# First norm's sums moved to TensorE and the last adaLN pair to VectorE in a one-core encoder layer

## The chip, the cores and the metric

The kernel runs on one core of one Trainium2 chip. The metric is device microseconds of one execution. Of the kernel before three runs were timed: 2474.91, 2477.87 and 2481.15 us, median 2477.87. One more execution was taken with the hardware profiler.

## The reference, cut to what matters

One encoder layer is applied to two requests of 256 tokens with D = 2048, laid side by side as 512 columns. The part around the change is the first adaLN-modulated RMSNorm and the product with `w_in`:

```
def rms_norm(x, g):
    y = x * rsqrt(mean(x * x, axis=-1, keepdims=True) + 1e-6)
    return y * g

def encoder_layer(x, c, w_ada, b_ada, norm1_g, w_in, ...):
    mod = silu(c) @ w_ada + b_ada                       # c: one row for each request
    sh1, sc1, gt1, sh2, sc2, gt2 = split(mod, 6)        # 2048 columns each
    hn = rms_norm(x, norm1_g) * (1 + sc1) + sh1
    h = hn @ w_in                                       # 6496 columns: RWKV-7 group, short-conv group
    ...                                                 # delta-rule scan in both directions, conv, gates
    x = x + gt1 * (concat([y_rwkv, y_conv]) @ w_out)
    hn = rms_norm(x, norm2_g) * (1 + sc2) + sh2
    ff = (silu(hn @ w_ffn_gate) * (hn @ w_ffn_up)) @ w_ffn_down
    return x + gt2 * ff                                 # and a last rms_norm
```

## The kernel before

Activations lie with features on the 128 partitions and the 512 tokens along the free axis, so x is 16 feature tiles `xt[k]` of 128x512. A product in nearly full precision is made of three matmuls of fp32r operands: each operand is split into a rounded high part and the low rest, and `products` issues high*high, high*low and low*high (a "group of three" below). The split of a 128x512 piece of weights is one ScalarE copy and one VectorE subtraction.

**The head** is the first 150 us or so. `ADA0` (line 42) lists the feature tiles of the first norm in the order in which their shift and scale columns of `w_ada` are worked out: tiles 0 and 1 alone, then six pairs, then tiles 14 and 15 alone. For each entry `ada_blocks` loads blocks of 512 KB into a ring of six buffers (g13, g14, g15, g18, g19, g20) and multiplies them by silu(c) in bank 6 (`ada_mm`); these are matmuls of plain fp32 with 32 rows of output. `ada_sum` copies the bank out with ScalarE and turns the sums into columns with small matmuls; `ada_mod` adds the biases (three small VectorE instructions into `md`) and then makes the two halves of `hn[k]`: two ScalarE activations of 128x256 with scale and bias, one ScalarE copy to the rounded part, one VectorE subtraction.

Between the entries stands `stream`, which multiplies the finished tiles with the 7 output tiles of `w_in0`: 7 groups of three matmuls for each feature tile, into 7 PSUM banks that stay open until tile 15. So the head holds 112 groups, and no bank can be read before tile 15 has been added. A raw block of `w_in0` holds 8 of these weights; there are three raw buffers and four buffers for split weights (h0 to h3).

`load_x` (line 662) loads x in eight pieces, squares each tile on ScalarE into two scratch halves of g9, and adds the squares up on VectorE into `sqa`, 15 additions one after the other. `rms` (line 564) sums `sqa` over the partitions with four matmuls against a column of ones, takes the root (one ScalarE instruction, some small VectorE instructions) and spreads the result over the partitions with four more matmuls. The result is copied to `rst`, and VectorE multiplies each of the 16 tiles by it in place.

**After the head** come eight passes over head pairs, each with a scan (`core`), with products of `w_in` as filling, then `w_out`, the second norm (`norm2`), the FFN and the last norm. Nine more groups of adaLN columns are worked out on VectorE meanwhile, 32 instructions each: `ada_rest` (line 759) loads `w_ada` in halves of 256 KB into `aw` and adds them, scaled by silu(c), into `aacc`; eight matmuls and a transposition then make columns of it (`asum`). The last of these groups is needed by `norm2`, whose tiles are made by `hn2_half` (line 1183) in one step: normed and scaled on VectorE, shifted and rounded on ScalarE, low part on VectorE.

**What sets the order.** Nothing is issued in the order of the code. All instructions are recorded as nodes with a cost and a priority (a lower number goes first); `Program.schedule` (line 239) runs a list scheduler over them and writes each engine's queue in the order of its planned starts. Each engine then works through its queue strictly in order, SyncE's queue of DMAs too. The planner holds a model of the DMA engines, one transfer after the other at 360 KB per us (line 328). Squares, the norm and the head's columns have priority 2 (`S_CORE`), splits of weights 0 (`S_SPLIT`), evacuations 1 (`S_EVAC`), VectorE's adaLN columns 8 (`S_ADA`), the groups of three 9 (`S_MAIN`).

Of the kernel before, what the change touches and what calls it, by code (L numbers as in the profile page):

```python
# [11 lines left out]
F32 = mybir.dt.float32  # L12
F32R = mybir.dt.float32r
AF = mybir.ActivationFunctionType
ALU = mybir.AluOpType
# [26 lines left out]
ADA0 = ((0, 1), (1, 1)) + tuple((k, 2) for k in range(2, 14, 2)) + ((14, 1), (15, 1))  # L42
# [154 lines left out]
class Program:  # L197
# [41 lines left out]
    def schedule(self):  # L239
# [24 lines left out]
        while done < n:  # L264
# [62 lines left out]
            if nbytes:  # L327
                dma_free = max(dma_free, end + 0.65) + nbytes / 360e3
                end = dma_free + 0.8
# [18 lines left out]
def hymba_layer_kernel(ctx: ExitStack, tc: tile.TileContext, xT, par, cst, w_ada0, w_ada1, w_in0, w_in1,  # L348
# [215 lines left out]
    def rms(sqacc, ps, psb, out, rs, prio, w0=0, w1=4):  # L564

        n = w1 - w0
        pe([mm(ps[:, w:w + 1], sqacc[:, 128 * w:128 * w + 128], ones, 1) for w in range(w0, w1)], prio)
        var, r, t = (rs[:, 4 * i + w0:4 * i + w1] for i in range(3))
        ts(var, ps[:, w0:w1], RMS_EPS, ALU.add, n, prio, fast=False)
        act(r, var, AF.Sqrt, n, prio)  # L570
        recip(r, r, n, prio)
        newton(r, var, t, n, prio)
        pe([mm(psb[:, 128 * w:128 * w + 128], r[:, w - w0:w - w0 + 1].to_broadcast([128, 128]), ident, 128)
            for w in range(w0, w1)], prio)
        if out is not None:
            acopy(out, psb, T, prio)
# [63 lines left out]

    def ada_mod(k0, nk):
        pt = bank[6]
        ada_sum(pt, g[11][:, 512 * (k0 // 2 % 2):512 * (k0 // 2 % 2) + 256 * nk], pt, 256 * nk, S_EVAC)
        m = pt[:, 0:4 * nk].rearrange("p (k a q) -> p a k q", a=2, q=2)
# [4 lines left out]
        for k in range(k0, k0 + nk):  # L649
            x, f = xt[k], g[10][:, 512 * (k % 2):512 * (k % 2) + 512]  # L650
            for q in range(2):
                s = slice(TQ * q, TQ * q + TQ)
                act(f[:, s], x[:, s], AF.Identity, TQ, S_EVAC, scale=md[:, 1, k, q:q + 1], bias=md[:, 0, k, q:q + 1])
            acopy(hn[k][:, 0:T], f, T, S_EVAC)
            tt(hn[k][:, T:], f, hn[k][:, 0:T].bitcast(F32), ALU.subtract, T, S_EVAC)
# [6 lines left out]
    def load_x():  # L662
# [3 lines left out]
        for k in range(KT):  # L666
            sumsq(xt[k], g[9][:, 512 * (k % 2):512 * (k % 2) + 512], sqa, k == 0, S_CORE)
        rms(sqa, bank[5], bank[5], rst, rs4, S_CORE)
        for k in range(KT):
            tt(xt[k], xt[k], rst, ALU.mult, T, S_CORE)  # L670
# [78 lines left out]
    for i, (k0, nk) in enumerate(ADA0):  # L749
        ada_blocks(k0, nk)  # L750
# [4 lines left out]
        ada_mod(k0, nk)  # L755
    stream(lambda i: w_in0[i], head, at=at, prio=S_HEAD)


    def ada_rest(gi, slots=None, prio=S_ADA):
# [9 lines left out]
        else:  # L769
            for kk in range(KT):  # L770
                w = wide["aw"][:, 512 * (kk % 2):512 * (kk % 2) + 512]
                dma(w, w_ada1[gi, kk // 2, :, 512 * (kk % 2):512 * (kk % 2) + 512], 1 << 18, S_ADA,
                    after=[hn[KT - 1]] if gi == 0 and kk < 2 else [])
                for q in range(2):
                    c = wide["aacc"][:, T * q:T * q + T]
                    if kk == 0:
                        ts(c, w, sil[:, kk, q:q + 1], ALU.mult, T, S_ADA)
                    else:
                        stt(c, w, sil[:, kk, q:q + 1], c, ALU.mult, ALU.add, T, S_ADA)
            a = wide["aacc"].rearrange("p (q j e i) -> p e q j i", q=2, j=4, e=4)  # L780
            pe([mm(ps[32 * e:32 * e + 32, 128 * q:128 * q + 128], unit, a[:, e, q], 128)
                for q in range(2) for e in range(4)], S_MISC)
            tr32(asum, ps[:, 0:256], 256, S_MISC)
# [809 lines left out]
```

## Time and profile before

| what | before |
|---|---|
| median of three runs | 2477.87 us |
| the profiled execution, its own time | 2481.56 us |
| its span, first to last instruction | 2479.7 us |
| TensorE busy | 2418.7 us, 98% |
| VectorE busy | 1911.8 us, 77% |
| ScalarE busy | 1112.5 us, 45% |
| share of TensorE in the chain that ended last | 86% |
| mean granted TensorE clock | 0.993 |

The span and what lies around it differ by 1.9 us. A busy TensorE is not TensorE at its peak, since the ends of matmuls are modelled; an idle stretch in brackets at the end of a timeline row names the engine and tile that ended it. In timeline rows `x8` counts records, and a plain fp32 matmul leaves two of them, so that four such matmuls read `x8` or somewhat less where a record is missing.

### The profile page before, as it was taken

The page shows a single profiled execution, that of the slowest core. Times are in us where ns is not written, and L with a number is a line of the kernel's source. Part 1 is how long each engine was busy: PE and PEld are TensorE (multiplying, and loading weights), DVE is VectorE, ACT ScalarE, POOL GpSimd, SP SyncE. Part 2 cuts the span into 40 slices and gives each one's busy share as a digit, 9 for nine tenths or more (in the row PEclk, how much of TensorE's full clock was granted, in tenths as well). Part 3 has the DMA queues.
Part 4 walks back from the last instruction along what each step waited for, and adds up shares of the span by engine and source line. Part 5 has one row for each costly group of instructions (what it writes and reads, how often), then busy time and mean ns, then how long its engine had stood idle before and what let it go on. Part 6 is the DMA issues. An engine that isn't in the chain of part 4 may idle for free.

```text
span 2479.7 us, 46341 instructions
## 1 busy us (share of the span) xinstructions
PE 2418.7 (98%) x18220; PEld 2066.7 (83%) x18220; DVE 1911.8 (77%) x3511; ACT 1112.5 (45%) x1848; POOL 12.5 (1%) x42
## 2 busy tenths in 40 slices
PE   5999999999999999989999999999999999999997
PEld 3578777777777777688999999999999988788887
DVE  4279988889889897795888888888888887734356
ACT  4465745745646643364444444444444433223232
POOL 0000000000000000000000000000000000000000
PEclk9999999999999999999999999999999999999998
DMA  9953434434434748733333333333333476533343
GB/s 344 357 163 125 146 120 135 148 130 138 152 119 141 235 133 285 273 109 103 128 112 128 120 120 120 117 122 114 126 111 128 161 230 201 197 112 127 120 139 115
DMA packets 188233, 384.66 MB, mean 155 GB/s; under 512 B 36336, under 2 KB 51056, under 8 KB 188016
## 3 DMA queue, kind: packets, MB, share of 16 engines
q1 hardware_dynamic: 188016, 381.72, 46.1%
q8 instruction: 142, 2.33, 0.4%
q14 instruction: 75, 0.61, 0.1%
HBM read 355.03 MB, written 28.18 MB: 155 GB/s over the span
## 4 chain that ended last, share of the span: by engine, by line
PE 86%; DVE 5%; DMA 5%; ACT 2%; issue 1%; SPq 0%; DVEq 0%; ACTq 0%
PE b L374 86%; DVE g L405 2%; DMA aw<-in_w_ada_dram 1%; ACT g L396 1%; DVE h L405 1%; DVE g L410 1%; DVE aacc L410 1%; DMA g<-hrvar 1%; DMA w<-in_w_out_dram 1%; PE b L385 1%; DMA g<-hrpre 1%; DMA w<-in_w_gu_dram 0%; DMA g<-hrmean 0%; ACT L396 0%; DMA hrmean<-rowm 0%
## 5 line engine op out<-in xcount | busy, mean ns | idle before, releaser
L374 PE MATMUL b<-r,h 128*128 128x512 f32 (+1 forms) x4920 | 1130.5, 375 | 4.8 <-ACT r L396 2.5
L374 PEld LDWEIGHTS b<-r,h 128*128 128x128 f32 x4920 | 856.1, 189 | 191.9 <-issue 28.8
L396 ACT ACTIVATE h<-w 128x512 fp32r<-128x512 f32 (+2 forms) x587 | 391.8, 670 | 643.2 <-PE b L374 572.9
L374 PE MATMUL b<-g,h 128*128 128x256 f32 (+1 forms) x3452 | 654.1, 332 | 0.5 <-DVE rowp L418 0.2
L405 DVE TENSOR_TENSOR h<-w,h 128x512 fp32r<-128x512 f32 (+3 forms) x595 | 432.6, 729 | 227.4 <-ACT h L396 215.1
L374 PEld LDWEIGHTS b<-g,h 128*128 128x128 f32 x3452 | 534.0, 190 | 73.8 <-issue 11.2
L374 PE MATMUL b<-g,g 128*128 128x256 f32 (+4 forms) x5372 | 427.2, 241 | 4.0 <-DVE g L405 2.9
L374 PEld LDWEIGHTS b<-g,g 128*128 128x128 f32 (+4 forms) x5372 | 354.1, 152 | 48.7 <-issue 25.6
L410 DVE SCALAR_TENSOR_TENSOR aacc<-aw,sil,aacc 128x512 f32<-128x512 f32 x390 | 276.5, 744 | 50.5 <-DMA aw<-in_w_ada_dram 49.2
L396 ACT ACTIVATE g<-g 128x1024 fp32r<-128x1024 f32 (+6 forms) x268 | 204.2, 763 | 247.0 <-DVE aacc L405 102.6
L405 DVE TENSOR_TENSOR g<-g,g 128x512 f32<-128x512 f32 (+24 forms) x681 | 253.8, 380 | 29.0 <-ACT g L396 12.8
L374 PE MATMUL b<-r,g 128*128 128x256 f32 x1412 | 269.5, 283 | 1.5 <-ACT r L396 1.3
L396 ACT ACTIVATE g<-b 32x128 f32<-32x128 f32 (+3 forms) x454 | 174.9, 390 | 167.3 <-PE b L374 141.2
L374 PEld LDWEIGHTS b<-r,g 128*128 128x128 f32 x1412 | 214.2, 191 | 1.9 <-ACT r L396 1.4
L374 PE MATMUL b<-g,r 128*128 128x256 f32 x748 | 194.7, 281 | 0.0
L374 PE MATMUL b<-r,r 128*128 128x256 f32 x700 | 189.0, 281 | 0.0
L405 DVE TENSOR_TENSOR g<-g,b 128x256 f32<-128x256 f32 (+1 forms) x300 | 146.1, 498 | 34.1 <-PE b L374 26.9
L405 DVE TENSOR_TENSOR r<-aacc,g 128x1024 fp32r<-128x1024 f32 x80 | 97.8, 1223 | 60.3 <-ACT g L396 60.3
L396 ACT ACTIVATE g<-aacc 128x1024 fp32r<-128x1024 f32 (+1 forms) x82 | 86.1, 1050 | 129.2 <-PE b L374 127.2
L405 DVE TENSOR_TENSOR r<-g,g 128x1024 fp32r<-128x1024 f32 x80 | 97.7, 1222 | 48.3 <-ACT g L396 48.3
L374 PEld LDWEIGHTS b<-g,r 128*128 128x128 f32 x748 | 134.2, 188 | 0.1
L374 PEld LDWEIGHTS b<-r,r 128*128 128x128 f32 x700 | 128.2, 188 | 0.0
(113 smaller groups left out, 1215.7 us busy)
## 6 DMA issues: line engine op xcount, KB each, us to landing
w<-in_w_gu_dram SPq DMA_DIRECT2D x240, 256.0 KB
aw<-in_w_ada_dram SPq DMA_DIRECT2D x208, 256.0 KB
w<-in_w_in_dram SPq DMA_DIRECT2D x102, 512.0 KB
w<-in_w_down_dram SPq DMA_DIRECT2D x88, 512.0 KB
g<-in_w_ada_dram SPq DMA_DIRECT2D x80, 512.0 KB
aw<-in_w_gu_dram SPq DMA_DIRECT2D x80, 256.0 KB
w<-in_w_out_dram SPq DMA_DIRECT2D x32, 512.0 KB
act<-g SPq DMA_DIRECT2D x44, 256.0 KB
```

The lines of the kernel that those rows point to most:

```text
L374: return [nc.tensor.matmul(R(out), lhsT=R(l), rhs=R(r), start=start, stop=stop) for out, l, r, n, start, stop, one in mms]
L385: return [nc.tensor.transpose(R(out), R(i), R(idn)) for out, i, idn in items]
L396: lambda: nc.scalar.activation(out=R(out), in_=R(in_), func=func, scale=R(scale), bias=R(bias)),
L405: lambda: e.tensor_tensor(out=R(out), in0=R(a), in1=R(b), op=op), [a, b], [out], prio)
L410: lambda: e.scalar_tensor_tensor(out=R(out), in0=R(a), scalar=R(s), in1=R(b), op0=op0, op1=op1),
```

## The change

- **Squares.** The squares of tiles 3, 6, 9, 11, 13 and 15 (`SQ_PE`) are no longer added on VectorE but summed over the partitions by TensorE, four matmuls against the column of ones for each tile, into the four columns of bank 5 that the sums of `sqa` go to; `rms` then adds those of `sqa` (`begun`). VectorE keeps 9 of the 15 additions. The scratch has four halves (g9 and g10) in place of two. `rms` of the first norm has priority 0 in place of 2.
- **One step.** The 16 multiplications of x by `rst` are gone. `ada_mod` makes each half tile with one VectorE instruction (x times scale times `rst`), one ScalarE activation (plus shift, rounded) and one VectorE instruction (low part), all of 128x256.
- **Tiles 14 and 15.** Their columns are worked out on VectorE by `ada_rows`, the code of `ada_rest` made common: 8 blocks of 512 KB into six buffers that the scan uses later (g12, g16, g17, g21, g22, g23), loaded at priority 8 once `hn[7]` is there, 32 instructions into `aacc`, then the eight matmuls and the transposition (`ada_columns`). The ring's matmuls for these two tiles are gone. The same bytes are loaded.
- **The list.** `ADA0` now has tiles 0 to 3 alone and then six pairs.
- **The planner** reckons with 390 KB per us in place of 360 for every DMA of the program, so that the order changes after the head too.

```diff
-ADA0 = ((0, 1), (1, 1)) + tuple((k, 2) for k in range(2, 14, 2)) + ((14, 1), (15, 1))
+ADA0 = ((0, 1), (1, 1), (2, 1), (3, 1)) + tuple((k, 2) for k in range(4, 16, 2))
+ADA0_DVE = {14: 7}
+SQ_PE = (3, 6, 9, 11, 13, 15)
...
-                dma_free = max(dma_free, end + 0.65) + nbytes / 360e3
+                dma_free = max(dma_free, end + 0.65) + nbytes / 390e3
...
-        pe([mm(ps[:, w:w + 1], sqacc[:, 128 * w:128 * w + 128], ones, 1) for w in range(w0, w1)], prio)
+        pe([mm(ps[:, w:w + 1], sqacc[:, 128 * w:128 * w + 128], ones, 1, not begun, not begun or w + 1 == w1)
+            for w in range(w0, w1)], prio)
...
+    def ada_rows(row, prio, after=(), blocks=None):
+        for kk in range(KT):
+            c = slice(512 * (kk % 2), 512 * (kk % 2) + 512)
+            if blocks is None:
+                w = wide["aw"][:, c]
+                dma(w, row(kk), 1 << 18, prio, after=after if kk < 2 else ())
+            else:
+                b = blocks[kk // 2 % len(blocks)]
+                w = b[:, c]
+                if kk % 2 == 0:
+                    dma(b, row(kk), 1 << 19, prio, after=after)
+            for q in range(2):
+                c = wide["aacc"][:, T * q:T * q + T]
+                if kk == 0:
+                    ts(c, w, sil[:, kk, q:q + 1], ALU.mult, T, prio)
+                else:
+                    stt(c, w, sil[:, kk, q:q + 1], c, ALU.mult, ALU.add, T, prio)
+    def ada_columns(ps, prio):
+        a = wide["aacc"].rearrange("p (q j e i) -> p e q j i", q=2, j=4, e=4)
+        pe([mm(ps[32 * e:32 * e + 32, 128 * q:128 * q + 128], unit, a[:, e, q], 128)
+            for q in range(2) for e in range(4)], prio)
+        tr32(asum, ps[:, 0:256], 256, prio)
     def ada_mod(k0, nk):
         pt = bank[6]
-        ada_sum(pt, g[11][:, 512 * (k0 // 2 % 2):512 * (k0 // 2 % 2) + 256 * nk], pt, 256 * nk, S_EVAC)
-        m = pt[:, 0:4 * nk].rearrange("p (k a q) -> p a k q", a=2, q=2)
+        if k0 in ADA0_DVE:
+            ada_columns(pt, S_EVAC)
+            m = asum.rearrange("p (q k a i) -> p a k q i", q=2, k=2, a=2)[:, :, :, :, 0]
+        else:
+            ada_sum(pt, g[11][:, 512 * (k0 // 2 % 2):512 * (k0 // 2 % 2) + 256 * nk], pt, 256 * nk, S_EVAC)
+            m = pt[:, 0:4 * nk].rearrange("p (k a q) -> p a k q", a=2, q=2)
...
-            x, f = xt[k], g[10][:, 512 * (k % 2):512 * (k % 2) + 512]
+            x, f = xt[k], g[9 + k // 2 % 2][:, 512 * (k % 2):512 * (k % 2) + 512]
             for q in range(2):
                 s = slice(TQ * q, TQ * q + TQ)
-                act(f[:, s], x[:, s], AF.Identity, TQ, S_EVAC, scale=md[:, 1, k, q:q + 1], bias=md[:, 0, k, q:q + 1])
-            acopy(hn[k][:, 0:T], f, T, S_EVAC)
-            tt(hn[k][:, T:], f, hn[k][:, 0:T].bitcast(F32), ALU.subtract, T, S_EVAC)
+                stt(f[:, s], x[:, s], md[:, 1, k, q:q + 1], rst[:, s], ALU.mult, ALU.mult, TQ, S_EVAC)
+                act(hn[k][:, s], f[:, s], AF.Identity, TQ, S_EVAC, bias=md[:, 0, k, q:q + 1])
+            for q in range(2):
+                s = slice(TQ * q, TQ * q + TQ)
+                stt(hn[k][:, T + TQ * q:T + TQ * q + TQ], f[:, s], md[:, 0, k, q:q + 1], hn[k][:, s].bitcast(F32),
+                    ALU.add, ALU.subtract, TQ, S_EVAC)
...
         for k in range(KT):
-            sumsq(xt[k], g[9][:, 512 * (k % 2):512 * (k % 2) + 512], sqa, k == 0, S_CORE)
-        rms(sqa, bank[5], bank[5], rst, rs4, S_CORE)
-        for k in range(KT):
-            tt(xt[k], xt[k], rst, ALU.mult, T, S_CORE)
+            t = g[9 + k // 2 % 2][:, 512 * (k % 2):512 * (k % 2) + 512]
+            if k in SQ_PE:
+                act(t, xt[k], AF.Square, T, S_CORE)
+                pe([mm(bank[5][:, w:w + 1], t[:, 128 * w:128 * w + 128], ones, 1, k == SQ_PE[0] and w == 0, False)
+                    for w in range(4)], S_CORE)
+            else:
+                sumsq(xt[k], t, sqa, k == 0, S_CORE)
+        rms(sqa, bank[5], bank[5], rst, rs4, S_SPLIT, begun=True)
...
-        ada_blocks(k0, nk)
+        if k0 not in ADA0_DVE:
+            ada_blocks(k0, nk)
...
+        for c, k in ADA0_DVE.items():
+            if k0 <= k < k0 + nk:
+                ada_rows(lambda kk: w_ada0[4 * c + kk // 2], S_ADA, [hn[k]], [g[i] for i in (12, 16, 17, 21, 22, 23)])
```

The queues that the change moves are shown at three places. In names, `g`, `h`, `b` and `r` with their first number are buffers, split weights, PSUM banks and tiles of `hn`; `x4` counts instructions.

TensorE's queue at the start, before: `g13` to `g20` are the ring's blocks times silu(c), `128x1` are the sums of the squares, `rs4` spreads the result, `r0` opens the products of tile 0.

```order
L374 MATMUL b6_293<-g13_243,sil32_205 32x256 x4
L374 MATMUL b5_298<-cs_199,g8_241 128x1 x4
L374 MATMUL b6_293<-g14_245,sil32_205 32x256 x4
L374 MATMUL b6_293<-g15_250,sil32_205 32x256 x4
L374 MATMUL b6_293<-g18_253,sil32_205 32x256 x4
L374 MATMUL b5_298<-cs_199,rs4_308 128x128 x4
L374 MATMUL b6_293<-cs_199,g11_330 32x2 x8
L374 MATMUL b6_293<-g19_256,sil32_205 32x256 x4
L374 MATMUL b6_293<-g20_260,sil32_205 32x256 x4
L374 MATMUL b6_293<-g13_243,sil32_205 32x256 x4
L374 MATMUL b0_385<-r0_374,h0_346 128x512 x3
L374 MATMUL b1_392<-r0_374,h0_346 128x512 x3
```

The same place after the change; ahead of it stand the sums of tiles 3, 6, 9, 11 and 13.

```order
L379 MATMUL b6_309<-g15_250,sil32_205 32x256 x4
L379 MATMUL b6_309<-g18_255,sil32_205 32x256 x4
L379 MATMUL b5_264<-cs_199,g10_252 128x1 x4
L379 MATMUL b5_264<-cs_199,g8_241 128x1 x4
L379 MATMUL b6_309<-cs_199,g11_333 32x2 x8
L379 MATMUL b6_309<-g19_258,sil32_205 32x256 x4
L379 MATMUL b6_309<-g20_261,sil32_205 32x256 x4
L379 MATMUL b5_264<-cs_199,rs4_348 128x128 x4
L379 MATMUL b6_309<-g13_243,sil32_205 32x256 x4
L379 MATMUL b6_309<-g14_246,sil32_205 32x256 x4
L379 MATMUL b6_309<-cs_199,g11_333 32x2 x8
L379 MATMUL b0_415<-r0_400,h0_364 128x512 x3
```

The last sums stood behind one of tile 0's four blocks and now stand behind all four; tile 0's products stood behind the third block of tile 1 and now stand behind its fourth and its sums. On VectorE the two low parts of `h0` and `h1` now stand between the small instructions of the root, where they stood behind them.

TensorE's queue from the column sums (`g11`, 32x2) of tiles 10 and 11 on, before, up to the tenth row after them; tile 10 follows after four more rows.

```order
L374 MATMUL b6_293<-cs_199,g11_330 32x2 x16
L374 MATMUL b7_456<-r8_822,h3_368 128x512 x3
L374 MATMUL b6_293<-g13_243,sil32_205 32x512 x2
L374 MATMUL b6_293<-g14_245,sil32_205 32x512 x2
L374 MATMUL b0_385<-r9_834,h3_368 128x512 x3
L374 MATMUL b1_392<-r9_834,h0_346 128x512 x3
L374 MATMUL b6_293<-g15_250,sil32_205 32x512 x2
L374 MATMUL b6_293<-g18_253,sil32_205 32x512 x2
L374 MATMUL b2_398<-r9_834,h0_346 128x512 x3
L374 MATMUL b3_409<-r9_834,h0_346 128x512 x3
L374 MATMUL b4_426<-r9_834,h0_346 128x512 x3
```

The same place after the change, to the first products of tile 10.

```order
L379 MATMUL b6_309<-g20_261,sil32_205 32x512 x2
L379 MATMUL b3_456<-r9_865,h0_364 128x512 x3
L379 MATMUL b4_471<-r9_865,h0_364 128x512 x3
L379 MATMUL b6_309<-cs_199,g11_333 32x2 x16
L379 MATMUL b5_264<-r9_865,h1_369 128x512 x3
L379 MATMUL b7_497<-r9_865,h1_369 128x512 x3
L379 MATMUL b0_415<-r10_1020,h1_369 128x512 x3
```

Two groups of three stand between the sums of tiles 10 and 11 and the first use of tile 10, where eight stood.

VectorE's queue around the last adaLN group (`aacc`, `asum`) and the second norm, before; `g21` with `r8` and bank 7 is the first tile of the second norm.

```order
L410 SCALAR_TENSOR_TENSOR aacc_1172<-aw_1150,sil_222,aacc_1172 128x512
L410 SCALAR_TENSOR_TENSOR g7_10045<-g20_260,md_342,g7_10045 128x256
L405 TENSOR_TENSOR aw_10049<-w2_270,aw_10049 128x512
L441 STREAM_TRANSPOSE asum_2193<-b5_298 128x256
L405 TENSOR_TENSOR md_342<-asum_2193,ba1_234 128x8
L405 TENSOR_TENSOR aacc_10061<-w2_270,aacc_10061 128x512
L405 TENSOR_TENSOR md_342<-md_342,pm_207 128x8
L410 SCALAR_TENSOR_TENSOR g21_1218<-r8_7855,md_342,b7_456 128x256
```

After the change; the root of the second norm's first half follows two rows further on.

```order
L415 SCALAR_TENSOR_TENSOR aacc_813<-aw_1208,sil_222,aacc_813 128x512
L410 TENSOR_TENSOR h2_373<-w1_273,h2_373 128x512
L410 TENSOR_TENSOR h3_377<-w1_273,h3_377 128x512
L410 TENSOR_TENSOR aw_9917<-w2_275,aw_9917 128x512
L415 SCALAR_TENSOR_TENSOR r15_8012<-b4_471,md_351,r15_8012 128x256
L410 TENSOR_TENSOR aacc_9933<-w2_275,aacc_9933 128x512
L410 TENSOR_TENSOR g23_790<-g23_790,g20_261 128x256
L446 STREAM_TRANSPOSE asum_1160<-b5_264 128x256
L410 TENSOR_TENSOR md_351<-asum_1160,ba1_234 128x8
L410 TENSOR_TENSOR md_351<-md_351,pm_207 128x8
```

The last column instruction and the transposition stood behind the root of the second norm's first half and behind tiles made from it; now they stand ahead of that root. On TensorE the group's eight matmuls stood right ahead of the sums of the second half; now they stand 14 rows ahead of the sums of the first half.

## Rows read from the trace of the kernel before

**Rows 1.** Busy time by stretch. Columns: the stretch in us from the span's start, its length, then busy time (and instructions) of TensorE, its weight loads, VectorE, ScalarE and GpSimd, then the granted TensorE clock as a share of full speed, the busy share of the DMA engines and GB/s.

```profile
0.00:30.00 30.00, 9.61 (x88) 5.58 (x88) 15.17 (x35) 16.97 (x29) 1.38 (x9) 1.00 0.95 364
30.00:54.00 24.00, 19.39 (x139) 9.97 (x139) 13.83 (x28) 8.12 (x16) 0.00 (x0) 0.92 0.94 335
54.00:155.00 101.00, 100.72 (x702) 60.56 (x703) 34.31 (x70) 41.83 (x74) 0.17 (x2) 0.99 0.80 290
155.00:1000.00 845.00, 832.34 (x7203) 648.65 (x7202) 736.62 (x1540) 471.25 (x933) 10.94 (x31) 1.00 0.49 155
1000.00:1100.00 100.00, 91.57 (x685) 73.25 (x684) 86.41 (x187) 47.04 (x98) 0.00 (x0) 0.95 0.62 211
```

**Rows 2.** The timeline of the first norm on all engines: start, duration, engine, line, operation, tiles, count of records, and in brackets the idle time before it and what ended it.

```profile
17.59 1.08 PE L374 MATMUL b<-g,sil 128*32 128x256 f32 x8 [17.59 <-DMA g<-in_w_ada_dram]
...
19.87 1.78 PEld L374 LDWEIGHTS b<-cs,g 128*128 128x128 f32 x8 [2.08 <-DVE g L405]
19.87 1.87 PE L374 MATMUL b<-cs,g 128*128 128x1 f32 x8 [1.20 <-DVE g L405]
...
23.02 0.16 DVE L405 TENSOR_TENSOR rs<-rs 128x4 f32<-128x4 f32 x1
...
24.39 2.06 PE L374 MATMUL b<-cs,rs 128*128 128x128 f32 x8
...
26.49 0.60 ACT L396 ACTIVATE g<-b 128x512 f32<-128x512 f32 x1 [1.58 <-PE b L374]
...
28.40 2.49 DVE L405 TENSOR_TENSOR h<-w,h 128x512 fp32r<-128x512 f32 x4
...
29.02 0.64 PE L374 MATMUL b<-g,sil 128*32 128x256 f32 x8 [0.84 <-DMA g<-in_w_ada_dram]
```

**Rows 3.** The same timeline from the first products on, with TensorE's idle stretches and VectorE's in-place scaling.

```profile
32.01 6.70 DVE L405 TENSOR_TENSOR g<-g,g 128x512 f32<-128x512 f32 x11
...
32.15 3.00 PE L374 MATMUL b<-r,h 128*128 128x512 f32 x8 [0.79 <-DVE r L405]
...
37.19 0.31 PE L374 MATMUL b<-cs,g 128*32 128x2 f32 x16
...
38.91 1.92 PE L374 MATMUL b<-g,sil 128*32 128x512 f32 x16 [0.51 <-DVE md L405]
...
50.18 0.43 PE L374 MATMUL b<-cs,g 128*32 128x2 f32 x32 [0.74 <-ACT g L396]
...
51.05 1.07 PE L374 MATMUL b<-g,sil 128*32 128x512 f32 x8 [0.43 <-DVE md L405]
...
53.36 0.69 DVE L405 TENSOR_TENSOR r<-g,r 128x512 fp32r<-128x512 f32 x1 [2.17 <-ACT r L396]
...
53.38 4.16 PE L374 MATMUL b<-r,h 128*128 128x512 f32 x9 [1.27 <-ACT r L396]
```

**Rows 4.** Granted clock of the stretch after the last of these idle times, in the columns of rows 1.

```profile
54.00:56.00 2.00, 1.90 (x5) 1.51 (x6) 0.74 (x2) 0.48 (x1) 0.00 (x0) 0.50 0.76 289
```

**Rows 5.** TensorE's timeline over a pair of tiles, over tiles 14 and 15 and at the end of the head (columns as in rows 2).

```profile
100.70 1.07 PE L374 MATMUL b<-g,sil 128*32 128x512 f32 x8
101.69 3.70 PE L374 MATMUL b<-r,h 128*128 128x512 f32 x15
...
122.82 1.07 PE L374 MATMUL b<-g,sil 128*32 128x256 f32 x16
...
125.40 0.64 PE L374 MATMUL b<-g,sil 128*32 128x256 f32 x8
...
126.86 0.64 PE L374 MATMUL b<-g,sil 128*32 128x256 f32 x8
...
128.32 0.31 PE L374 MATMUL b<-cs,g 128*32 128x2 f32 x16
...
136.58 17.97 PE L374 MATMUL b<-r,h 128*128 128x512 f32 x78
```

**Rows 6.** Prices on VectorE and TensorE that the new instructions are nearest to: the first two rows are forms of VectorE's line 410 (count, shortest, median and longest duration in ns), the last is TensorE's timeline at one group's eight column matmuls.

```profile
L410 DVE SCALAR_TENSOR_TENSOR aacc<-aw,sil,aacc x390: 647/745/754, 145.6 to 2154.9; 128x512 f32<-128x512 f32 x195
...
L410 DVE SCALAR_TENSOR_TENSOR r<-g,md,r x16: 464/476/483, 1073.9 to 1098.0; 128x256 fp32r<-128x256 f32 x16
...
  DMA aw<-in_w_ada_dram: 49.2, 53
...
255.61 0.62 PE L374 MATMUL b<-aacc,cs 128*32 128x128 f32 x16
```

**Rows 7.** TensorE's timeline at the second norm (columns as in rows 2), and under the dots the granted clock of one stretch in the columns of rows 1.

```profile
1079.56 0.43 PE L374 MATMUL b<-aacc,cs 128*32 128x128 f32 x8 [0.34 <-DVE aacc L410]
1081.93 0.43 PE L374 MATMUL b<-aacc,cs 128*32 128x128 f32 x8 [1.94 <-DVE aacc L410]
1083.67 0.61 PE L374 MATMUL b<-cs,g 128*128 128x1 f32 x4 [1.32 <-DVE asum L441]
1085.61 0.58 PE L374 MATMUL b<-r,g 128*128 128x256 f32 x1 [1.33 <-ACT r L396]
1086.38 3.99 PE L374 MATMUL b<-r,g 128*128 128x256 f32 x17 [0.19 <-DVE r L410]
...
1090.88 3.84 PE L374 MATMUL b<-r,g 128*128 128x256 f32 x30
...
1086.00:1088.00 2.00, 1.81 (x8) 1.62 (x8) 2.00 (x9) 2.00 (x7) 0.00 (x0) 0.50 0.59 223
```

More of the change, by code (lines that the diff above doesn't have):

```diff
@@ L561, in mtile, with rms @@
                  (lambda: done(ps)) if k == n - 1 else None) for k in range(n)]
-    def rms(sqacc, ps, psb, out, rs, prio, w0=0, w1=4):
+    def rms(sqacc, ps, psb, out, rs, prio, w0=0, w1=4, begun=False):
         n = w1 - w0
-        pe([mm(ps[:, w:w + 1], sqacc[:, 128 * w:128 * w + 128], ones, 1) for w in range(w0, w1)], prio)
+        pe([mm(ps[:, w:w + 1], sqacc[:, 128 * w:128 * w + 128], ones, 1, not begun, not begun or w + 1 == w1)
+            for w in range(w0, w1)], prio)
         var, r, t = (rs[:, 4 * i + w0:4 * i + w1] for i in range(3))
@@ L769, in ada_rest @@
         else:
[L770 to L783, printed above, removed]
+            ada_rows(lambda kk: w_ada1[gi, kk // 2, :, 512 * (kk % 2):512 * (kk % 2) + 512], S_ADA,
+                     [hn[KT - 1]] if gi == 0 else ())
+            ada_columns(ps, S_MISC)
         kind, k0 = 2 + gi // 4, 4 * (gi % 4)
```

## The prediction, made before the changed kernel ran

> **What bounds the kernel now.** I first read busy time by stretch [rows 1]. From 155 us on TensorE is idle for 12.7 of 845 us up to 1000 and for 8.4 of the 100 us after that. In the head it is idle for 20.4 of the first 30 us and 4.6 of the next 24, and then for 0.3 of 101. The DMA engines are 95, 94 and 80% busy in these three stretches: transfers set the first 30 us, and TensorE's own work sets the head from 54 us on. So the change can gain by an earlier start, by less TensorE work in the head, by closing the holes between 30 and 54 us, and by one other hole, the second norm.
>
> I then read the timeline of the norm [rows 2]: the sums at 19.87, the root until 23.18 (23.02 + 0.16), the spread 24.39 to 26.45, its copy out until 27.09. In [rows 3] the first full burst of products starts at 32.15, and after it TensorE waits 0.51, 0.74, 0.43 and 1.27 us for `md` and for tiles behind it on VectorE, which is then scaling eleven tiles of x in place, 6.70 us in a row. After the 1.27 the granted clock is 0.50 [rows 4], the lower of its two levels. The last products of the head end at 136.58 + 17.97 = 154.55 [rows 5], 122.4 us after 32.15.
>
> The sum is made against the profiled execution, 2481.56 us, and the difference is then taken from the median, 2477.87, which is 3.7 lower. A measurement of this kernel can tell about 0.3% from no change, here 2470.4 to 2485.3.
>
> **The change part by part.**
>
> (a) *Start.* TensorE waited for block 1 of `w_ada` until 17.59 and for the seventh block, which reuses its buffer, until 29.02 [rows 2]. Nine transfers of 512 KB lie between them in SyncE's queue (six blocks and three of `w_in0`): 1.27 us each. So tile 0's fourth block lands at about 21.4. In the new queue the last sums stand behind all four blocks of tile 0. A block takes 0.64 to 1.08 us of TensorE [rows 2], I take 0.9, so these sums start at 22.3. They are now eight matmuls in place of four: 2 x 1.87 = 3.74, to 26.0, where it was 21.74. The root took 1.44 (21.74 to 23.18), and two of the four low parts of `h` (2.49 / 4 = 0.62 each) now stand between its instructions: 28.7. Spread 2.06, copy 0.60: 31.4. A tile is then two VectorE instructions of 0.48 [rows 6] and a ScalarE one of about 0.5 (estimated from the 0.60 of a 128x512 copy). Tile 1's last block and column sums now stand ahead of the first product. First burst: 33.5, **1.35 late**. Were the sums to run at the pace of the second norm, 0.61 for four records [rows 7], it would be 31.5; with tile 0's blocks late by one transfer it would be 35.
>
> (b) *TensorE's work after the start.* Tiles 14 and 15 each leave 1.00 + 0.57 + 0.57 + 0.24 = 2.38 (the rows 1.07, 0.64, 0.64 and 0.31 of [rows 5], less the 0.07 by which a row overlaps the next): -4.75. Tiles 2 and 3 taken singly cost 2 x 2.38 in place of four blocks of 1.00 and sums of 0.36 (the 0.43 of [rows 3], less 0.07): +0.39. Tile 1's last block and sums now lie ahead of the start: 1.0 + 0.25 = -1.25. The new pair's eight column matmuls cost what such a group costs [rows 6]: +0.62. Sum **-5.0**.
>
> (c) *Holes.* 0.51 + 0.74 + 0.43 + 1.27 = 2.95, and nine products at the lower clock took 4.16 where fifteen at the higher took 3.70 [rows 5], 2.22 for nine: 1.9 more. With no scaling on VectorE, tiles 2 to 4 stand free well before TensorE asks for them: **-4.75** (-2.5 if half of the holes stay).
>
> (d) *New wait at tile 10.* Between the column sums of tiles 10 and 11 and tile 10's products stood eight groups of three and four blocks; now there are two groups, 6 x 0.245 = 1.5 us. The way from sums to a finished tile was 50.18 to 53.36 + 0.69 = 54.05 [rows 3], 3.9 us. TensorE runs its queue strictly in order, so every later tile stands behind this. **+2.5**; 0 if ScalarE and VectorE have nothing queued ahead, up to 6 if VectorE's column instructions stand ahead and the clock falls as it did at 54 us.
>
> Head: 33.5 + 122.4 - 5.0 - 4.75 + 2.5 = 148.7 in place of 154.55, **-5.9** (bounds -10.4, from an early start and no wait at tile 10, and -0.6, from a late start and the full wait).
>
> (e) *What costs nothing, and by which cover.* The 32 column instructions of tiles 14 and 15 cost 32 x 0.745 = 23.8 us of VectorE [rows 6], but it is busy for 34.3 of 101 us [rows 1]. The one-step tiles exchange 0.69 for 0.96 of VectorE; same cover. The same bytes are loaded, and tiles 14 and 15 need theirs only at the end of the head. In SyncE's queue these eight loads come behind the ring's. If the cover is gone, tile 14 is late, and TensorE waits at the end of the head; some 19 of 112 groups stand between, so I give it nothing. Six fewer additions on VectorE shorten no path, since x lands after them one tile at a time.
>
> (f) *Second norm.* Before, TensorE waited 0.34 for `aacc`, 1.94 for it again, 1.32 for `asum` and 1.33 for a tile [rows 7], 4.93 in all, and then ran at 0.50: seventeen products took 3.99 where thirty took 3.84, 1.7 more. Now the last column instructions and the transposition stand ahead of the root, and TensorE's eight matmuls fourteen rows ahead of the first half's sums. The two waits for `aacc` (2.28) may stay, since VectorE has as much to do there as before; the rest goes: **-4.3** (0 if VectorE is what is late, -7 if all goes).
>
> *The scan.* The planner's 256 KB transfer shrinks by 56 ns (0.728 to 0.672), and the queues of the passes are re-mixed. Before, VectorE waited 49.2 us for `aw` in 53 waits [rows 6], without TensorE being idle for more than 12.7 [rows 1]. I take **0**, within 4 either way, a third of that idle time.
>
> The sum is -5.9 - 4.3 = **-10.2**: 2471.4 beside 2481.56, and 2467.7 beside the median. I say 2468.
>
> The Trainium skill ("TensorE: Matmul & The Clock Gate", section "LDWEIGHTS (loading the stationary operand)") puts a weight load at its columns over 1.2 ns, 107 ns for 128. Eight loads of the norm's sums took 1.78 us, 222 ns each [rows 2], so the row differs from the page by a factor of two. An estimate by the page has the eight sums' sixteen loads done in 1.7 us, and the total at 2466.
>
> **The rivals.**
>
> *Quick sums, no wait at tile 10.* The sums take 0.15 us a record as at 1083.67 [rows 7], 2.4 in place of 3.74 with less queued behind, and ScalarE and VectorE are idle when tile 10 comes. For it: VectorE is only a third busy there. Against: 1.87 is what this very step took in its place. About 4.5 less: 2463.
>
> *The head gives nothing.* The longer sums, the wait at tile 10 and a clock that falls there eat (b) and (c). For it: two more waits in series ahead of the first product, and DMA at 95%. Against: 5 us of TensorE's work are really gone. Only (f) is left: 2473.6.
>
> *Second norm unmoved.* The last `aacc` instruction waits for its half of `w_ada`, not for its place. For it: both `aacc` waits end on VectorE, which waits for such loads. The price is all of (f): 2472.
>
> *Slower: loads planned too fast.* At 390 KB per us the planner lets VectorE's column instructions stand earlier in its queue than their data are there; VectorE, strictly in order, then holds splits and scan steps behind them, and TensorE waits. For it: 49.2 us of such waits already, hidden only because TensorE has work in stock. Against: DMA is 49% busy in that stretch. It decides when TensorE's idle time from 155 to 1000 us grows from 12.7 past 30 (2467.7 + 17.6 = 2485.3); at 32 it gives 2487.
>
> **How the numbers follow.** Forecast 0.50 (2463 to 2473), quick sums 0.13, the head gives nothing 0.18, second norm unmoved 0.12, slower 0.07. Faster by over 0.3%, below 2470.4: all of quick sums, 0.35 of the forecast's 0.50, 0.09 from the two at 2472 to 2474, together 0.57. Slower 0.07. Within: 0.36. The range: the head's bounds (4.5 down, 5.3 up), the second norm's (2.7 down, 4.3 up) and the scan's 4 are independent, so root of squares: 6.6 down, 7.9 up. It is stretched by 2 for the ends of the two rivals at 2463 and 2473.6: 2459 to 2477, which leaves out the slower case and some 0.06 on each side.
>
> **What would show it.** Right: eight sums at 22 to 26, first burst near 33.5, no idle stretch from there to 105, a gap of 1 to 4 us near 107 to 110 ended by a tile behind `md`, last head products ending near 148.7; at the second norm no waits for `asum` and no clock of 0.50; 10 to 16 us of idle TensorE from 150 to 1000. Wrong: a first burst after 35, a wait for tile 14's `aacc` near 130, the clock at half around tile 10, or new waits of TensorE for splits in the scan, with VectorE waiting for `aw` ahead of them.

## The result: 0.8% slower, and the profile after

Four runs of the changed kernel gave a median of 2500.42 us (2495.86 to 2504.99), beside 2479.51 us for the kernel before: ratio 1.0081, 95% interval 1.0062 to 1.0101. The forecast was 2468, range 2459 to 2477. The profiled execution has a span of 2494.8 us (before 2479.7).

Busy time by stretch of the changed kernel, in the columns of [rows 1]:

```profile
0.00:30.00 30.00, 18.38 (x132) 14.46 (x136) 11.13 (x30) 15.79 (x28) 1.38 (x9) 0.92 0.95 361
30.00:54.00 24.00, 23.25 (x187) 11.68 (x180) 9.52 (x27) 6.60 (x14) 0.00 (x0) 0.81 0.98 381
54.00:155.00 101.00, 98.69 (x634) 62.59 (x633) 69.56 (x141) 36.53 (x65) 0.16 (x2) 0.98 0.76 283
155.00:1000.00 845.00, 823.81 (x7147) 639.46 (x7145) 731.20 (x1533) 467.22 (x925) 10.51 (x31) 0.99 0.49 154
1000.00:1100.00 100.00, 91.51 (x672) 71.74 (x673) 79.71 (x169) 41.47 (x83) 0.00 (x0) 0.98 0.64 217
1100.00:2494.80 1394.80, 1375.44 (x9457) 1276.47 (x9456) 1033.16 (x1675) 534.06 (x720) 0.00 (x0) 0.99 0.40 132
```

The last stretch before:

```profile
1100.00:2479.70 1379.70, 1365.03 (x9408) 1268.72 (x9406) 1025.45 (x1657) 527.27 (x702) 0.00 (x0) 1.00 0.40 133
```

Read each row's length less TensorE's busy time. Up to 54 us the idle time fell from 25.0 [rows 1] to 12.4 us, and from 54 to 155 it rose from 0.3 to 2.3. From 155 to 1000 it rose from 12.7 to 21.2, from 1000 to 1100 it stayed (8.4 and 8.5), and behind 1100 it rose from 14.7 to 19.4.

TensorE's timeline in the head of the changed kernel, in the columns of [rows 2], [rows 3] and [rows 5]:

```profile
21.69 2.26 PE L379 MATMUL b<-cs,g 128*128 128x1 f32 x32
...
26.66 2.07 PE L379 MATMUL b<-cs,rs 128*128 128x128 f32 x8 [1.19 <-DVE rs L410]
29.73 1.08 PE L379 MATMUL b<-g,sil 128*32 128x256 f32 x8 [1.00 <-DMA g<-in_w_ada_dram]
...
32.96 4.21 PE L379 MATMUL b<-r,h 128*128 128x512 f32 x9
...
109.34 0.43 PE L379 MATMUL b<-cs,g 128*32 128x2 f32 x32
...
112.42 0.50 PE L379 MATMUL b<-r,h 128*128 128x512 f32 x1 [1.06 <-ACT r L401]
113.46 3.31 PE L379 MATMUL b<-r,h 128*128 128x512 f32 x8 [0.54 <-DVE r L415]
...
131.28 19.13 PE L379 MATMUL b<-r,h 128*128 128x512 f32 x83 [0.54 <-DVE r L415]
150.58 9.12 PE L379 MATMUL b<-r,h 128*128 128x512 f32 x39 [0.17 <-DVE g L415]
```

The first burst starts at 32.96 (forecast 33.5, before 32.15); no idle stretch follows until 112; the wait at tile 10 is 1.06 + 0.54. The products before the last row end at 131.28 + 19.13 = 150.41, where 154.55 stood [rows 5]: the head gained 4.1 us. The last row is a mark that every run has, 39 products in one piece right behind the head. It starts at 150.58; before, at 154.73. From this mark to the end of the span the kernel before takes 2325.0 us and the changed one 2344.2: **19 us are lost behind the head.**

Where they go is seen on VectorE. Its waits in the changed kernel (engine and tile that waits, what for, us in total, times, longest):

```profile
DVE aacc L415 <- DMA aw<-in_w_ada_dram: 65.6, 59, 6.0
...
DVE g L415 <- DMA g<-hrvar: 12.3, 4, 5.4
DVE g L415 <- DMA g<-hrmean: 11.0, 6, 3.9
```

Before, `aacc` waited 49.2 us for `aw`, 2.4 at the longest [rows 6 for the total], and `hrvar` (a small piece of the scan that goes through DRAM and back) cost 7.9. A stretch of the changed kernel's chain of waits shows how such a wait comes to TensorE (start, us, what):

```profile
930.37 4.44 DMA aw<-in_w_ada_dram
...
934.91 0.75 DVE aacc L415
935.66 0.34 DVE g L410
...
936.03 0.42 ACT g L401
936.46 0.04 issue
936.50 3.63 PE b L379 x55
```

What TensorE does at 936.50 needs no `aacc`. But VectorE works in order: the small `g` of the scan at 935.66 stands behind a column instruction that stands behind a load, and ScalarE and TensorE wait for that `g`. TensorE has other products in stock and is idle for only 0.60 us here. Its longest idle stretch in the scan looks otherwise. First TensorE's timeline at both places, then the chain at the second:

```profile
936.50 1.85 PE L379 MATMUL b<-g,g 128*64 128x64 f32 x48 [0.60 <-ACT g L401]
...
679.75 0.43 PE L379 MATMUL b<-g,cs 128*32 128x64 f32 x16 [3.04 <-ACT g L401]
...
674.37 3.88 DMA g<-hrmean
...
678.34 0.70 DVE g L415
679.04 0.02 issue
679.07 0.64 ACT g L401
```

Here the chain waits for a round trip through DRAM and not for `aw`. Between 155 and 1000 us the changed kernel has eight idle stretches of TensorE of 0.9 us or more, 15.7 us in all, and each, followed back, comes to something that returns from DRAM (`hrvar`, `hrmean`, `hrpre`, `vrev`, `yc`). Before there were three such, 5.8 us in all, and one of 1.48 us behind `aw`.

### The profile page after: what moved, and what is told of

It reads as the page before. It is cut to its first block, busy times and chain, and to the rows that moved or that the text cites. A ratio compares the mean times of both kernels' runs of the same rounds, so it can differ in the third digit from the quotient of the medians.

```text
span 2494.8 us, 46416 instructions
## 1 busy us (share of the span) xinstructions
PE 2431.1 (97%) x18220; PEld 2076.4 (83%) x18220; DVE 1934.3 (78%) x3570; ACT 1101.7 (44%) x1832; POOL 12.0 (0%) x42
## 4 chain that ended last, share of the span: by engine, by line
PE 81%; DMA 9%; DVE 6%; issue 2%; ACT 1%; SPq 0%; DVEq 0%; ACTq 0%
PE b L379 80%; DMA aw<-in_w_ada_dram 4%; DVE aacc L415 2%; DVE g L410 1%; DVE h L410 1%; DVE g L415 1%; DMA g<-hrpre 1%; DMA r<-act 1%; ACT g L401 1%; PE b L390 1%; DMA g<-hrmean 1%; DMA g<-in_w_ada_dram 1%; DMA w<-in_w_out_dram 1%; SPq L443 0%; DVE r L415 0%
## 5 line engine op out<-in xcount | busy, mean ns | idle before, releaser
L410 DVE TENSOR_TENSOR g<-g,g 128x512 f32<-128x512 f32 (+24 forms) x659 | 240.0, 371 | 32.0 <-ACT g L401 17.7
```

Of the source, the lines that this page charges most:

```text
L410: lambda: e.tensor_tensor(out=R(out), in0=R(a), in1=R(b), op=op), [a, b], [out], prio)
```

## The experiments

Three theories. **A:** the planner's 390 KB per us has VectorE's instructions planned ahead of their data, as in the rival "loads planned too fast". **B:** the new column group on VectorE pushes the nine later groups back. **C:** any re-mixing of the queues is a draw of some 15 us. Ratios are to the kernel before in the same set of runs, with 95% intervals; five rounds each.

**e1 and e2: the planner's figure alone, undone and done.**

```diff
 e1, changed kernel
-                dma_free = max(dma_free, end + 0.65) + nbytes / 390e3
+                dma_free = max(dma_free, end + 0.65) + nbytes / 360e3
 e2, kernel before
-                dma_free = max(dma_free, end + 0.65) + nbytes / 360e3
+                dma_free = max(dma_free, end + 0.65) + nbytes / 390e3
```

> The changed kernel with the planner's figure put back to 360 KB per us; nothing is left out. Theory A (loads planned too fast): with the old figure the idle time of TensorE from 155 to 1100 us falls back from 30 to about 21 us and the gain of the head (4 us) and of the second norm stay: 2468 to 2474. Theory B (the adaLN columns of tiles 14 and 15 on VectorE push the nine later groups back): the planner's figure does not matter, 2492 to 2504. Theory C (each re-mixing of the queues after the head is a draw that can cost or give some 15 us, with no cause in the loads): anywhere from 2465 to 2500, and not explained by VectorE's waits for aw.

> The kernel before with only the planner's figure raised to 390 KB per us; nothing is left out. Theory A: some 19 us slower than before, 2490 to 2500, with more waits of VectorE for aw. Theory B: as before, 2475 to 2482. Theory C: within 15 us of before on either side, unrelated to e1.

e1: 2479.67 us, ratio 1.0006 (0.9997 to 1.0015). e2: 2497.64 us, ratio 1.0085 (1.0071 to 1.0099). So the one figure, put into the kernel before with nothing else, makes the whole loss, and B falls. In e1 TensorE's idle time from 155 to 1100 us is back at 20.7, as A has it. But e1 does not reach A's 2468 to 2474: with the old figure norm and columns together gain nothing. And e2 had a surprise: its mark behind the head starts at 150.28, 4.4 us earlier than before, with neither new norm nor new columns. In e1 it starts at 155.20. **The figure alone gives the head as much as the whole change does**, though not in the same way, as (b) and (c) below show.

**e3 and e4: norm alone, columns alone, at 360.** e3 is the changed kernel with the old `ADA0` and no `ADA0_DVE`; e4 is the changed kernel with the old `load_x` and the old tile code in `ada_mod`.

> The changed norm alone: six tiles' squares summed on TensorE, tiles scaled in one step; the old list of adaLN tiles, tiles 14 and 15 by the ring, planner's figure 360. Theory A: the head ends 2 to 3 us earlier than before (the holes between 34 and 54 us gone, the work of tiles 14 and 15 still there), the total 2474 to 2478. Theory B: the same, 2472 to 2478. Theory C: anywhere within 15 us of 2476.

> The new list and the columns of tiles 14 and 15 on VectorE alone, with the old norm and the planner's figure 360. Theory A: 3 to 5 us of TensorE's work leave the head, total 2472 to 2478. Theory B: the later adaLN groups start some 24 us of VectorE time later, TensorE waits for aacc at the ends of groups, 2488 to 2500. Theory C: anywhere within 15 us of 2476.

e3: 2478.55 us, ratio 0.9999 (0.9989 to 1.0010). e4: 2474.91 us, ratio 0.9983 (0.9973 to 0.9993). So e4 is where A and C put it, B falls again, and e3 is half a microsecond above A's 2474 to 2478. Both heads moved by about a microsecond (marks at 153.59 and 153.82). That is no more than a spread of executions: before, e6, e9, e10 and e12 have one and the same order up to 350 us, and their marks lie from 153.87 to 155.35. In e1, TensorE and VectorE around tile 10 show where the head's gain went. TensorE of e1:

```profile
110.97 0.43 PE L379 MATMUL b<-cs,g 128*32 128x2 f32 x32 [0.70 <-ACT g L401]
116.88 1.93 PE L379 MATMUL b<-g,sil 128*32 128x512 f32 x8 [5.47 <-DVE md L410]
118.74 3.34 PE L379 MATMUL b<-r,h 128*128 128x512 f32 x6
```

VectorE of e1 in the same stretch:

```profile
108.65 8.03 DVE L415 SCALAR_TENSOR_TENSOR aacc<-g,sil,aacc 128x512 f32<-128x512 f32 x12
116.60 0.15 DVE L410 TENSOR_TENSOR md<-b,pm 128x4 f32<-128x4 f32 x1
```

Twelve column instructions of tiles 14 and 15 stand ahead of the `md` of the pair that TensorE waits for: a wait of 5.47 us, and six products behind it take 3.34 us, about twice their time at the higher clock. e4 has the same wait (3.83).

**e5 and e6: where in the program the figure acts.** The figure depends on the planned start `s` of the transfer.

```diff
 e5, changed kernel
-                dma_free = max(dma_free, end + 0.65) + nbytes / 390e3
+                dma_free = max(dma_free, end + 0.65) + nbytes / (390e3 if s < 155 else 360e3)
 e6, kernel before
-                dma_free = max(dma_free, end + 0.65) + nbytes / 360e3
+                dma_free = max(dma_free, end + 0.65) + nbytes / (360e3 if s < 155 else 390e3)
```

> The changed kernel with 390 KB per us for transfers that are planned to start in the first 155 us and 360 for all later ones; nothing is left out. Theory A (past the head, loads are planned earlier than they land): the head ends near 150.5 us as in the changed kernel, and from there the time is that of e1: 2473 to 2478, VectorE's waits for aw near 48 us. Theory C (each mixing is a draw): within 15 us of 2480, and VectorE's waits for aw tell nothing.

> The kernel before with 360 KB per us in the first 155 us of the plan and 390 for all later transfers; nothing is left out. Theory A: the head as before, all of the loss after it: 2495 to 2504, VectorE's waits for aw 65 us or more. Theory C: within 15 us of 2480.

e5: 2475.48 us, ratio 0.9977 (0.9968 to 0.9986), mark at 150.35, VectorE's wait for `aw` back to 52.2. e6: 2503.89 us, ratio 1.0096 (1.0078 to 1.0113), head as before (mark 155.35). VectorE's waits in e6:

```profile
DVE aacc L410 <- DMA aw<-in_w_ada_dram: 75.4, 63, 5.8
...
DVE g L410 <- DMA g<-hrvar: 14.2, 4, 5.0
```

Both fell where A put them.

**e7 and e8: other figures, kernel before (330 and 420 in place of 360).**

> The kernel before with the planner's figure at 330 KB per us; nothing is left out. Theory A: loads are planned later than they land, VectorE's waits for aw fall below 49 us, the time after the head is no longer than before: 2470 to 2484, the head itself up to 5 us longer. Theory C: within 15 us of 2480 on either side.

> The kernel before with the planner's figure at 420 KB per us; nothing is left out. Theory A: worse than at 390, as the waits for aw grow further: 2500 to 2520. Theory C: within 15 us of 2480 on either side, not ordered by the figure.

e8: 2512.94 us, ratio 1.0128 (1.0111 to 1.0145), as A has it, and `aw` cost 86.0:

```profile
DVE aacc L410 <- DMA aw<-in_w_ada_dram: 86.0, 70, 5.3
```

So 360, 390 and 420 stand in order in time (1, 1.0085, 1.0128) and in waits for `aw` (49.2, 70.3, 86.0), which a draw would hardly do. e7, however, is slower as well: 2487.11 us, ratio 1.0029 (1.0019 to 1.0040), 5.6 us, beyond A's 2470 to 2484. Its waits for `aw` did not fall (52.3). The products behind its head start at 158.66, so 3.9 us lie in the head, within the 5 that A allowed. Behind the head TensorE's timeline of e7 has one long wait:

```profile
158.66 8.44 PE L374 MATMUL b<-r,h 128*128 128x512 f32 x36 [0.17 <-DVE g L410]
...
1091.15 1.32 PE L374 MATMUL b<-aacc,cs 128*32 128x128 f32 x16 [15.83 <-DVE aacc L410]
```

The last adaLN group comes late for the second norm, which waits 15.83 us for it (before 0.34 and 1.94 [rows 7]). That it is late because its loads were planned later is argued from this one trace and was not tried. Of the four figures 360 is the fastest.

**e9, e10 and e12: which loads.** e9 is e6 with most loads of the later groups cut short, which leaves out the columns of these groups, e10 the kernel before with the same cut; the order on TensorE, VectorE and ScalarE is that of e6 and of before. e12 raises the price of these loads alone.

```diff
 e9, e10
-                dma(w, w_ada1[gi, kk // 2, :, 512 * (kk % 2):512 * (kk % 2) + 512], 1 << 18, S_ADA,
+                n = 512 if kk < 2 else 32
+                dma(w[:, 0:n], w_ada1[gi, kk // 2, :, 512 * (kk % 2):512 * (kk % 2) + n], 1 << 18, S_ADA,
 e12, kernel before
-                dma_free = max(dma_free, end + 0.65) + nbytes / 360e3
+                dma_free = max(dma_free, end + 0.65) + nbytes / (390e3 if s >= 155 and prio == 8 else 360e3)
```

> The kernel of e6 (before, with 360 KB per us for the head and 390 after it), same order on TensorE, VectorE and ScalarE, but 14 of 16 loads of each later adaLN group bring 32 of 512 columns, so that the columns of these groups are left out; the loads land early and VectorE hardly waits for aw. Theory A1 (the loss is VectorE standing in order behind aw): the penalty of 22 us of e6 against before goes, and e9 is within 6 us of e10. Theory A2 (the loss is other loads planned too early: weights of w_in and w_out, the small round trips of the scan): e9 stays 15 to 22 us above e10.

> Control of e9: the kernel before with the same loads cut and the same columns left out. Theory A1: VectorE's 49 us of waits for aw go and TensorE's idle time after the head falls a little: 2460 to 2475. Theory A2: 2470 to 2480, e9 far above it.

> The kernel before with 390 KB per us only for the loads of the later adaLN groups, 360 for all others; nothing is left out. Theory A1 (aw planned too early is enough): 10 to 20 us slower than before, waits for aw 60 us or more. Theory A2 (the rest of the loads): within 5 us of before. Since transfers are planned one after the other, a part of the loss may stay with the other loads: 5 to 10 us would mean that both count.

e9: 2475.67 us, ratio 0.9983 (0.9974 to 0.9992). e10: 2467.21 us, ratio 0.9943 (0.9931 to 0.9954). The same order that cost 22.4 us (e6 less before, 2503.89 - 2481.49) costs 8.5 when the loads are short: 14 of 22 us go with the bytes of these loads, be it that VectorE stands behind `aw` or that the loads keep other transfers waiting. That lies between A1 (within 6) and A2 (15 to 22). What the other 8 are is not shown, for the short loads did not end VectorE's waits for `aw`, in e9 and e10:

```profile
DVE aacc L410 <- DMA aw<-in_w_ada_dram: 30.8, 39, 5.3
...
DVE aacc L410 <- DMA aw<-in_w_ada_dram: 18.7, 25, 2.4
```

e12: 2488.53 us, ratio 1.0040 (1.0026 to 1.0055), 8.4 us, `aw` at 63.1; the expectation had named 5 to 10 us as the sign that both kinds of load count. Of the other kind the round trips of the scan are seen: VectorE's waits for loads that return through DRAM, added up behind 155 us, were 18.8 us before, 31.5 in e6, 27.1 in e9 and 33.9 in the changed kernel. That these make the 8 us was not tried by itself.

**e11, e13 and e14: 390 for the head, 360 behind it, with each part of the change.** Same edit of the planner's line as in e5: e13 in the kernel before, e14 with the norm alone (as e3), e11 with the columns alone (as e4).

> A version made to beat both: e4 (the columns of tiles 14 and 15 on VectorE and the new list, old norm) with 390 KB per us in the first 155 us of the plan and 360 after; nothing is left out. Theory A: the head gains some 4 us as in e2 and e5, the rest as in e4: 2468 to 2473. Theory C (each mixing is a draw): 2465 to 2490.

> The kernel before with 390 KB per us in the first 155 us of the plan and 360 after; nothing is left out. If the head's gain came from the planner's figure alone: first pass of the scan near 192 us as in e2, total 2474 to 2478. If it came from norm and columns: 2478 to 2482, as before.

> The changed norm alone (old list, tiles 14 and 15 by the ring) with 390 KB per us in the first 155 us of the plan and 360 after; nothing is left out. If the new norm is worth nothing beside the figure: as e13 within 3 us. If it costs, as the step from e11 to e5 suggests: 4 to 8 us above e13. If it gives the 2 to 3 us of closed holes that the prediction had: that much below e13.

| 390 for the head only | old columns | new columns |
|---|---|---|
| old norm | e13: 2477.81, 0.9994 (0.9984 to 1.0005), mark 150.97 | e11: 2467.93, 0.9949 (0.9935 to 0.9963), mark 149.35 |
| new norm | e14: 2473.05, 0.9973 (0.9961 to 0.9986), mark 152.29 | e5: 2475.48, 0.9977 (0.9968 to 0.9986), mark 150.35 |

e13: the head's 3.8 us came with the figure alone, though the total moved by less than can be told. e14 was expected within 3 us of e13, 4 to 8 above it or 2 to 3 below; it is 4.8 below. **e11 beats both kernels**: the columns with the old norm, 12 us under before. The parts don't add: norm alone takes 0.2%, columns alone 0.45%, both 0.17%. At the mark all four lie within 3 us, so most of these differences arise behind the head, where the order is mixed anew for each. In the stretch of [rows 1] from 1000 to 1100, e11 has this row:

```profile
1000.00:1100.00 100.00, 97.71 (x739) 78.76 (x737) 85.99 (x193) 54.29 (x117) 0.00 (x0) 1.00 0.55 188
```

2.3 us of idle TensorE where before has 8.4, and the clock at 1.00. e4 and e14 come to 2.2 and 2.0, e13 to 4.1, e5 and the changed kernel only to 7.6 and 8.5.

All runs together speak against C as the cause of the loss. The five kernels with 390 or more behind the head (the changed one, e2, e6, e8, and e12 for some loads) are 0.4 to 1.3% slower than before. The other seven with 360 there (e1, e3, e4, e5, e11, e13, e14) have ratios from 0.9949 to 1.0006, and none is slower beyond its interval. These seven still lie up to 12 us apart, which is what the mixing alone can do. But VectorE's wait for `aw` does not part the two lots. In e13 and e14 it is as long as in the changed kernel, and they lose nothing:

```profile
DVE aacc L410 <- DMA aw<-in_w_ada_dram: 67.8, 53, 4.6
...
DVE aacc L415 <- DMA aw<-in_w_ada_dram: 65.1, 58, 3.3
```

VectorE's waits for round trips behind 155 us do so only nearly: 16.2 to 25.5 us in the seven, 24.2 to 33.9 in the five.

## Why the prediction was wrong, point by point

**The failed step** is the term behind (f), "*The scan* ... I take **0**, within 4 either way". From the mark on it measured +19 in the changed kernel, +20 in e2 and +22 in e6. I priced the figure by what it does to one transfer, 56 ns, and held the waits for `aw` to be hidden since TensorE was idle so little. Both were wrong in kind: the figure decides which instructions and transfers are put ahead of which, and each one put ahead of its data holds all that stands behind it. The 49.2 us of waits were also misread, since 21.3 of them lie behind 1100 us and so were never covered by the 12.7 of idle time up to 1000.

That the figure makes the loss behind the head is shown (e2, e5 and e6). It stood among the rivals ("loads planned too fast") at 0.07. The path that this rival drew is shown only in part. The bytes of the adaLN loads carry 14 of e6's 22 us (e9), and the sign to watch, VectorE's wait for `aw`, did grow in every kernel that lost. But it grew as much in e13 and e14, which lost nothing, and TensorE's longest idle stretches up to 1000 us come from round trips through DRAM, which the prediction did not name. The rival's place was drawn too narrowly too. Idle time from 155 to 1000 us reached 21, not 30. Of the 13.3 us of idle time that came in from 155 us on, 4.7 lie behind 1100, where TensorE waits 4.2 us for `aacc` (1.0 before, 7.5 in e6). Some of the rest of the 19 went in stretches at the lower clock: the mean is 0.99 there, before 1.00.

**(a) Start: right in time, for the wrong reason in part.** 33.5 forecast, 32.96 measured. The eight sums took not 3.74 but about 1.95 us (the 2.26 of the first row above, which also holds 16 records of column sums, 0.31 in [rows 3]); the time went into waits for `rs`, for the block at 29.73 and a clock of 0.50, by which the first nine products took 4.21 us. (The 31.5 that the prediction gives for the quick pace does not follow from its terms: sixteen records at 0.15 save 1.3 us, which makes 32.2.)

```profile
32.00:37.00 5.00, 4.44 (x29) 3.12 (x25) 2.15 (x7) 1.29 (x3) 0.00 (x0) 0.50 1.02 407
```

**(b) and (c), -5.0 and -4.75: the holes close, but at 360 the head ends no earlier.** The holes between 34 and 54 us are gone, as forecast (the terms of (c) add up to 4.85, not 4.75). Norm and columns close them without the figure: e1 is not idle at all from 30 to 54 us, while e2, with the figure alone, still waits 0.90, 0.43, 1.27 and 0.23 us there. Here e1, e2, and e1 further on:

```profile
30.00:54.00 24.00, 24.00 (x198) 13.51 (x191) 9.91 (x27) 7.13 (x16) 0.00 (x0) 1.00 0.97 370
...
30.00:54.00 24.00, 20.54 (x155) 11.35 (x152) 14.30 (x29) 8.62 (x16) 0.00 (x0) 1.00 1.01 397
...
100.00:125.00 25.00, 18.79 (x112) 8.93 (x111) 20.93 (x38) 4.35 (x9) 0.00 (x0) 0.80 0.88 333
```

e1 loses its gain again: 2.3 us of waits between 62 and 67 us, then 0.70 and 5.47 at tile 10, with a mean clock of 0.80 from 100 to 125 us. e2 gains elsewhere: its first burst starts at 31.23, 0.9 us earlier than before, and its clock stays at 1.00 to the end of the head. In e11 against e13 the columns are worth 1.6 us of the head, not 5, and that is about the spread of single executions.

**(d) Wait at tile 10: right in place, 1.6 for 2.5** in the changed kernel, and 5.47 in e1, by the very cause named for the upper bound: VectorE's column instructions stand ahead. The clock fell there too: its mean from 100 to 125 us is 0.93 in the changed kernel, one of the signs of being wrong that the prediction named. So the cover of part (e), "busy for 34.3 of 101 us", was the wrong test: a third busy on average, VectorE is busy for 8 us in a row just where a tile is due.

**The head as a sum: -5.9 forecast, -4.1 measured**; sign and size held, its causes only in part, since the figure alone gave as much. (The upper bound of -0.6 is -0.9 by the terms that it names, 1.5 for the start and 3.5 for the wait.)

**(f) Second norm, -4.3: not seen.** The changed kernel is idle for 8.5 us there, before 8.4. TensorE's timeline after:

```profile
1036.85 2.78 PE L379 MATMUL b<-g,sil 128*32 128x512 f32 x24 [1.59 <-DVE md L410]
...
1075.77 0.43 PE L379 MATMUL b<-aacc,cs 128*32 128x128 f32 x8 [3.02 <-DVE aacc L415]
1076.77 0.66 PE L379 MATMUL b<-aacc,cs 128*32 128x128 f32 x8 [0.57 <-DVE aacc L415]
```

The waits for `asum` are gone, as forecast. But the eight matmuls now wait for `aacc` ahead of the first half's sums, 3.02 + 0.57, and other waits of 1.59 and 1.66 (for `md` and `aacc`) came in earlier: the end "0 if VectorE is what is late". The clock of 0.50 [rows 7] is not gone but stands right behind these waits, in the columns of [rows 1]:

```profile
1077.00:1079.00 2.00, 2.00 (x15) 1.65 (x8) 1.46 (x3) 2.00 (x4) 0.00 (x0) 0.50 0.00 0
```

That less idle time was to be had there is shown by e4, e11 and e14, but not by the way of (f). In these the eight matmuls stand behind the first half's sums, as before, and `aacc` is done by then. e13 has the order of (f) and still waits 1.12 and 0.63 us for `aacc`.

**What stays open.** Why norm and columns, each a gain with 390 for the head, gain no more together: the four kernels differ behind the head by the mixing of their queues, and no run separates that. Nor is it shown how much of the loss reaches TensorE through VectorE standing behind `aw`, and how much through round trips that land late among the loads: e9 shortens the loads and so eases both.

## What to carry to other kernels

A constant in a scheduler's model is a change to every queue of the program. Price it by which instructions and transfers it puts ahead of others, not by the nanoseconds that it takes off one transfer. Look for the waits that are hidden so far on an engine that works in order, and ask what stands behind them; then follow the bottleneck's own idle stretches back, for the longest list of waits need not be what it waits for. Undo the one-line part of a large change first, and try it by itself in the old kernel: two runs told here that it makes the whole loss, and by itself as much gain in the head as the whole change. Work moved onto an engine "with room" is judged by what stands ahead of the next due instruction, not by the busy share.

## What the runs showed of the hardware that was not expected

The same matmuls of the squares (128x1, fp32, loads of 128 columns) ran at two paces. In TensorE's timeline of the changed kernel, 32 records took 7.16 us while x was coming in, 224 ns each, as the eight before had done in [rows 2]; the last sixteen took about 1.95 us, 122 ns each; in e1, sixteen at the same place took 3.58 us, 224 ns each (the second row):

```profile
10.87 7.16 PE L379 MATMUL b<-cs,g 128*128 128x1 f32 x32 [0.37 <-ACT g L401]
...
19.77 3.58 PE L379 MATMUL b<-cs,g 128*128 128x1 f32 x16
```

The granted clock read 1.00 in all three places. The Trainium skill ("TensorE: Matmul & The Clock Gate", section "LDWEIGHTS (loading the stationary operand)") gives 107 ns for 128 columns: the faster pace comes near it, the slower is twice that, and no run here shows what sets it.
